# Encoder layer on one core: constant products ahead of the first loads, the first root in one run, and the last output block's sums and scalings on other engines

## The chip, the cores and the metric

The kernel runs on one core of a Trainium2 chip. The metric is the device time of one execution in microseconds (us), as the median of several runs. Five engines work side by side, each through a list of instructions of its own: TensorE (PE; its weight loads are PEld), VectorE (DVE), ScalarE (ACT), GpSimd (POOL) and SyncE (SP), which issues most of the DMAs. All data are float32; PSUM has eight banks for the results of products, and SBUF holds everything else.

## The reference

A layer of a bidirectional encoder on 2048 tokens of 1024 channels. Cut to what matters here:

```python
u = rms_norm(h, norm_mix_g) ; proj = u @ w_in        # the opening of the kernel
h = h + concat(hyena(proj), mlstm(proj)) @ w_out
h = h + cross_attention(rms_norm(h, norm_x_g), rms_norm(mem, norm_mem_g))
h = h + square(relu(rms_norm(h, norm_ff_g) @ ff_w1)) @ ff_w2
return rms_norm(h, final_norm_g)                     # the end of the kernel
```

`rms_norm(x, g)` is `x * rsqrt(mean(x * x) + eps) * g` over the 1024 channels.

## The kernel before, in words

**Products.** Every operand of a product is split into a high and a low half of a shorter type (ScalarE copies the high half, L1667 or L368, and VectorE or GpSimd subtracts it, L1668 or L368). A product of two split operands is three matmuls (`mm3`: L357 high by high, L360 and L361 with one low half each). A scheduler orders each engine's instructions from estimates of its own; an instruction given to `keep_in_program_order` (in `x_first` it is called `pin`) stays in the order of the code, and `behind` puts one behind the last product written so far.

**Opening** (`x_first`, L543 to L640, and `sweep`). The first projection needs x of 512 tokens times the gain, in halves (xh by ScalarE L574, xl by VectorE L575), for the first half x0 and then for the next 512 tokens x1. The norm's root is not applied to the operands: it multiplies the results. For it, ScalarE squares x (L580), VectorE adds the eight squares up (L582, `ssum`), TensorE adds over the channels (`columns`, L587, four products with a column of ones), VectorE takes the inverse root (`inv_rms` L462, `rsqrt` L230 to L234, a copy L463) and spreads it over a diagonal (L496), TensorE makes rows of it (`rows`, L598, ones times diagonal), ScalarE copies them (`rowb`, L599), and VectorE multiplies the results with them (L780). `sweep` makes one group of 24 products (eight k by three) after another, first two columns of the first weight block with x0, two of the second block with x0, and then the same four with x1. `self.made` counts the groups; `hooks` is a table that says before which group and k each part above is written down. L278 is the first product of the filters' small network, which runs between the groups. The halves of a later weight block are made by L368.

**Last block** (`ffn`, from L1777). The second projection of the feed-forward part uses seven products per block of 2 by 2 in place of eight. It has four blocks o of output columns; for each, the products i come in the order 1, 6, 7, 5, 3, 2, 4 (`ORDER_DOWN`), for two halves tp of the tokens, with four steps k of 12 matmuls. `fetch_a` prepares the weight side (ah, al; for i = 3 it first subtracts one block from another, L1795) and `fetch_b` the activation side (bh, bl). After the last step of a product its four banks are added to `acc[i, tp]` (L1994, VectorE). Banks come in two sets of four, `mm` for tp = 0 and `hy` for tp = 1. Only in the last block, o = 3, `add(i, j, tp, engine)` then adds the accumulators to each other (L1960), four pieces each, which makes the four output blocks of the scheme. `turned` queues the transposes of the finished blocks (L1927), whose results are squared by ScalarE (L1929) and multiplied with the final gain by VectorE (L1930), and `finish` takes the root and scales both halves of 512 tokens c (L1942 on VectorE for h = 1 and even c, L1944 on ScalarE otherwise) and stores them (L1947). The order of c is 1, 3, 0, 2; c = 0 and c = 2 end the kernel.

Of the kernel before, what the change touches and what calls it, by code (L numbers as in the profile page):

```python
# [10 lines left out]
F32 = mybir.dt.float32  # L11
# [3 lines left out]
ALU = mybir.AluOpType  # L15
# [5 lines left out]
D = 1024  # L21
# [112 lines left out]
class Prog:  # L134
# [88 lines left out]

    def rsqrt(self, pool, ms, name):
        nc = self.nc
        shp = list(ms.shape)
        y = pool.tile(shp, F32, tag=name + "_y", name=name + "_y", bufs=2)
        t = pool.tile(shp, F32, tag=name + "_t", name=name + "_t", bufs=2)
        yi, mi = y.bitcast(I32), ms.bitcast(I32)
        nc.vector.tensor_scalar(yi, mi, -0.5, float(0x5F3759DF), ALU.mult, ALU.add)  # L230
        for _ in range(3):
            nc.vector.tensor_tensor(t, y, y, ALU.mult)
            nc.vector.scalar_tensor_tensor(t, t, -0.5, ms, ALU.mult, ALU.mult)
            nc.vector.scalar_tensor_tensor(y, t, 1.5, y, ALU.add, ALU.mult)  # L234
        return y
# [222 lines left out]

    def inv_rms(self, dst, src):
        nc, sb, n = self.nc, self.isb, dst.shape[1]  # L460
        ms = sb.tile([128, 4], F32, tag="ms", name="ms", bufs=2)[:, 0:n]
        nc.vector.tensor_scalar(ms, src, 1.0 / D, EPS, ALU.mult, ALU.add)  # L462
        nc.vector.tensor_copy(dst, self.rsqrt(sb, ms, "xr"))  # L463

# [27 lines left out]

    def diagonal(self, cols):
        dg = self.isb.tile([128, 512], F32, tag="rb", name="dg", bufs=2)[:, 0:128 * cols.shape[1]]
        for t in range(cols.shape[1]):
            self.nc.vector.tensor_scalar(dg[:, 128 * t:128 * t + 128], self.ident, cols[:, t:t + 1], None, ALU.mult)  # L496
        return dg
# [50 lines left out]
    def x_first(self):  # L548
# [22 lines left out]
        def operand(xs, c, k):  # L571
            to = (slice(None), k, slice(512 * c, 512 * c + 512))
            g = self.g_mix[:, k:k + 1]
            pin(nc.scalar.activation(self.xh[to], xs[k], AF.Copy, scale=g))  # L574
            nc.vector.scalar_tensor_tensor(self.xl[to], xs[k], g, self.xh[to].bitcast(F32), ALU.mult, ALU.subtract)  # L575

        def squares(xs, c):
            for k in range(8):
                sq = sb.tile([128, 512], F32, tag="st", name="sq", bufs=3) if k else ssum[c]
                pin(nc.scalar.activation(sq, xs[k], AF.Square))  # L580
                if k:
                    nc.vector.tensor_tensor(ssum[c], ssum[c], sq, ALU.add)  # L582

        def columns(c):
            p = self.hy()
            for t in range(4):
                d = nc.tensor.matmul(p[:, t:t + 1], ssum[c][:, 128 * t:128 * t + 128], self.ones[:, 0:1], start=True, stop=True)  # L587
# [33 lines left out]

        def halfway():
            operands(range(4, 8))
            squares(x1, 1)
# [114 lines left out]
    def sweep(self, cols, hf, first, after=None):  # L739
# [3 lines left out]
        for run in [cols[:2]] + [[c2] for c2 in cols[2:]] if self.made == 0 else [[c2] for c2 in cols]:  # L743
# [7 lines left out]
            for c, c2 in [(c, c2) for c in range(2) for c2 in run]:  # L751
                wh, wl = ws[c2]
                for m in range(2):
# [5 lines left out]
                    for k in range(8):  # L759
                        if (self.made, k) in self.hooks:  # L760
                            self.hooks.pop((self.made, k))()
                            hook = True
                        else:
                            hook = False
                        self.mm3(p, wh[:, k, ms], wl[:, k, ms], xh[:, k, cs], xl[:, k, cs], k == 0, k == 7,
                                 k == 0 and 3 < self.made < 13 or hook and self.made in (2, 3))

# [1004 lines left out]
    def ffn(self):  # L1772
# [127 lines left out]
        with tc.tile_pool(name="down", bufs=1) as B:  # L1900
# [31 lines left out]
            def finish(c, dst):  # L1932
                m = B.tile([128, 4], F32, tag="mo", name="mo", bufs=2)
                q = self.rbp[:, 4 * c:4 * c + 4]
                for h in range(2):
                    nc.vector.scalar_tensor_tensor(m, ss[:, c, h], 1.0 / D, m if h else q, ALU.mult, ALU.add)
                rv = self.rsqrt(B, m, "or")
                for t in range(4):
                    for h in range(2):
                        v = dst[h][:, t]  # L1940
                        if h and c % 2 == 0:
                            nc.vector.tensor_scalar(v, v, rv[:, t:t + 1], None, ALU.mult)  # L1942
                        else:
                            nc.scalar.mul(v, v, rv[:, t:t + 1])  # L1944
# [13 lines left out]
            def add(i, j, tp, eng):  # L1958
                for m in range(4):
                    eng.tensor_tensor(acc[i, tp][:, m], acc[i, tp][:, m], acc[j, tp][:, m], ALU.add)  # L1960

            early = [(i, tp, k) for i in (7, 4, 3, 2) for tp in range(2) for k in range(4)]
            outs = []
            V, G = nc.vector, nc.gpsimd
            for s, (n, tp, k) in enumerate(down):
# [17 lines left out]
                if tp and n + 1 < len(prods):  # L1983
                    fetch_a(n + 1, k)
                for _ in range(min(len(outs), 2 if len(outs) > 4 or n + 1 == len(prods) else 1)):
                    outs.pop(0)("mm" if tp else "hy")
                if k < 3:
                    continue
                for m in range(4):
                    v = acc[i, tp][:, m]  # L1990
                    if o == 0 and i in (1, 6, 5):
                        nc.scalar.copy(v, bank[m])
                    else:
                        d = nc.vector.tensor_tensor(v, bank[m], v, ALU.add)  # L1994
                        if s + 1 == len(down):
                            tc.keep_in_program_order(d)
                if o < 3:
                    continue
# [4 lines left out]
                elif i == 7:  # L2003
                    add(7, 6, tp, V)
                    add(3, 6, tp, G)
                elif i == 5:
                    add(3, 5, tp, V)
                    add(5, 7, tp, G)
                    add(4, 7, tp, G)
                    if tp:  # L2010
                        outs += turned(1, 0, 1, 5, 1)
                elif i == 3:
                    c = 2 * tp + 1
# [3 lines left out]
                elif i == 2:  # L2017
                    outs += turned(2 * tp, tp, 0, 2, 7)
                elif i == 4:
# [129 lines left out]
```

## Time and profile before

| | us |
|---|---|
| median of 3 runs | 3109.32 (3107.85 to 3111.45) |
| profiled execution | 3110.14 |
| its span on the core | 3108.4 |
| TensorE busy | 3025.3 (97%) |
| VectorE busy | 1955.3 (63%) |
| ScalarE busy | 1497.7 (48%) |
| GpSimd busy | 1141.1 (37%) |

A row of the timeline has the start in the span, the duration, the engine, the line, the operation, what it writes and reads, shapes, how many such instructions stand in a row (x), and in brackets the idle time just before with what ended it. A row of a group has the number, the busy time, the mean duration of one in ns, and the idle time. A row of windows has the busy time of each engine in that stretch with its number of instructions, the granted clock of TensorE (PEclk, 1.00 is full), the share of the DMA engines' time and the rate. Matmuls are pipelined, so the time that one takes is read from start to start.

### The profile page before, as it was taken

How to read it: one execution, taken by the hardware profiler on the slowest of the kernel's cores; microseconds unless marked ns; L12 is line 12 of the kernel's file. 1: busy time of each engine (PE TensorE's matmuls, PEld its weight loads, DVE VectorE, ACT ScalarE, POOL GpSimd, SP SyncE). 2: the span in 40 equal slices, each digit the busy share in tenths (PEclk: the TensorE clock that was granted, in tenths of full speed). 3: DMA queues.
4: the chain of work that ended last, by engine and by line, in shares of the span. 5: the costliest groups of instructions: out<-in, count | busy, mean ns of one | idle time of the engine just before them, and what ended most of it. 6: DMA issues, size and time to landing. Idle time of an engine off the chain costs nothing.

```text
span 3108.4 us, 42926 instructions
## 1 busy us (share of the span) xinstructions
PE 3025.3 (97%) x14257; PEld 2374.5 (76%) x14257; DVE 1955.3 (63%) x3429; ACT 1497.7 (48%) x2931; POOL 1141.1 (37%) x802
## 2 busy tenths in 40 slices
PE   8999999999999998999999999999999999999998
PEld 6655667776676766888887888888888788888876
DVE  7865465446756456877664566657554676565696
ACT  6543466533656225565544455556555443333335
POOL 0122011200222333333132337766466375243693
PEclk9999999999999999999999999999999999999999
DMA  6654768576878996565476557657644565354435
GB/s 211 190 198 163 231 207 251 178 232 194 254 203 241 302 300 220 158 199 170 143 250 206 197 172 235 207 178 238 200 153 153 171 210 182 109 166 118 157 93 172
DMA packets 444102, 607.07 MB, mean 195 GB/s; under 512 B 38494, under 2 KB 248542, under 8 KB 442856
## 3 DMA queue, kind: packets, MB, share of 16 engines
q1 hardware_dynamic: 405988, 546.54, 55.2%
q10 hardware_dynamic: 37892, 57.79, 5.5%
q8 instruction: 113, 1.85, 0.2%
q14 instruction: 109, 0.89, 0.1%
HBM read 401.79 MB, written 202.41 MB: 194 GB/s over the span
## 4 chain that ended last, share of the span: by engine, by line
PE 55%; DVE 3%; DMA 1%; issue 1%; ACT 1%; POOL 0%; SPq 0%; DVEq 0%; POOLq 0%; ACTq 0%
PE mm L361 12%; PE mm L357 12%; PE mm L360 12%; PE hy L357 6%; PE hy L361 6%; PE hy L360 6%; DVE bl L1668 1%; PE hy L1310 1%; PE hy L1312 1%; DVE acc L1960 0%; PE hy L1458 0%; DVE acc L1994 0%; PE hy L1571 0%; DMA va<-vd 0%; PE hy L1272 0%
## 5 line engine op out<-in xcount | busy, mean ns | idle before, releaser
L1668 DVE TENSOR_TENSOR bl<-wr,bh 128x512 fp32r<-128x512 f32 x213 | 242.1, 1142 | 127.6 <-ACT bh L1667 122.9
L1667 ACT CAST ah<-w 128x512 fp32r<-128x512 f32 x284 | 176.5, 622 | 301.1 <-PE hy L360 155.9
L368 DVE TENSOR_TENSOR wl<-wn,wh 128x512 fp32r<-128x512 f32 (+1 forms) x296 | 213.1, 765 | 101.0 <-ACT wh L368 100.4
L357 PE MATMUL mm<-xh,wh 128*128 128x512 f32 x640 | 267.5, 419 | 8.5 <-ACT wh L368 7.9
L1024 POOL TENSOR_TENSOR b<-b,a 128x512 f32<-128x512 f32 x64 | 87.0, 1362 | 509.4 <-ACT b L1022 238.8
L360 PE MATMUL mm<-xl,wh 128*128 128x512 f32 x640 | 253.7, 397 | 1.3 <-DVE xl L368 1.3
L361 PE MATMUL mm<-xh,wl 128*128 128x512 f32 x640 | 254.8, 399 | 0.0
L1667 ACT CAST bh<-wr 128x512 fp32r<-128x512 f32 x232 | 143.5, 621 | 230.2 <-PE mm L361 172.6
L1668 DVE TENSOR_TENSOR al<-w,ah 128x512 fp32r<-128x512 f32 x236 | 216.0, 916 | 55.5 <-ACT ah L1667 54.1
L357 PE MATMUL mm<-bh,ah 128*128 128x512 f32 x576 | 225.2, 391 | 1.8 <-DVE acc L1830 1.7
L361 PE MATMUL mm<-bh,al 128*128 128x512 f32 x576 | 223.3, 390 | 2.6 <-POOL al L1668 2.6
L360 PE MATMUL mm<-bl,ah 128*128 128x512 f32 x576 | 224.4, 390 | 0.0
L368 ACT CAST wh<-wn 128x512 fp32r<-128x512 f32 (+1 forms) x296 | 164.2, 618 | 109.4 <-PE mm L361 52.7
L360 PE MATMUL mm<-act,wh 128*128 128x512 f32 x512 | 202.3, 395 | 0.0
L361 PE MATMUL mm<-act,wl 128*128 128x512 f32 x512 | 200.5, 393 | 0.9 <-DVE wl L368 0.9
L357 PE MATMUL mm<-act,wh 128*128 128x512 f32 x512 | 199.6, 396 | 1.3 <-ACT wh L368 1.2
L357 PE MATMUL hy<-bh,ah 128*128 128x512 f32 x448 | 175.2, 391 | 0.0
L360 PE MATMUL hy<-bl,ah 128*128 128x512 f32 x448 | 174.6, 390 | 0.0
L361 PE MATMUL hy<-bh,al 128*128 128x512 f32 x448 | 174.4, 390 | 0.0
L357 PEld LDWEIGHTS mm<-xh,wh 128*128 128x128 f32 x640 | 121.1, 189 | 60.8 <-issue 18.6
L357 PE MATMUL mm<-wh,xh 128*128 128x256 f32 (+1 forms) x512 | 156.0, 305 | 3.8 <-ACT xh L368 2.3
L361 PEld LDWEIGHTS mm<-xh,wl 128*128 128x128 f32 x640 | 121.0, 189 | 47.8 <-issue 23.2
(375 smaller groups left out, 8225.4 us busy)
## 6 DMA issues: line engine op xcount, KB each, us to landing
wr<-hc SPq DMA_DIRECT2D x224, 256.0 KB
w<-in_ff_w_dram SPq DMA_DIRECT2D x172, 256.0 KB
hc<-wn SPq DMA_DIRECT2D x128, 256.0 KB
wn<-in_w_in_dram SPq DMA_DIRECT2D x100, 256.0 KB
hc<-q SPq DMA_DIRECT2D x96, 256.0 KB
fs<-a SPq DMA_DIRECT2D x32, 512.0 KB
a<-fs SPq DMA_DIRECT2D x64, 256.0 KB
a<-zs SPq DMA_DIRECT2D x64, 256.0 KB
```

The costliest lines, as they stand in the source:

```text
L357: first = mm(ps, lh, rh, start=start, stop=False)
L360: mm(ps, lh, rl, start=False, stop=False)
L361: self.last = mm(ps, ll, rh, start=False, stop=stop)
L368: both = (self.nc.scalar.copy(hi, src), self.nc.vector.tensor_tensor(lo, src, hi.bitcast(F32), ALU.subtract))
L1024: nc.gpsimd.tensor_tensor(xt, xt, hi[:, m], ALU.mult)
L1310: nc.tensor.matmul(dst, nm[:, h], va[:, h], start=True, stop=state is None)
L1312: nc.tensor.matmul(dst, rows_[d, 1][:, h], state[:, h], start=False, stop=True)
L1667: self.nc.scalar.copy(hi, src)
L1668: eng.tensor_tensor(lo, src, hi.bitcast(F32), ALU.subtract)
```

## The change

**Opening.** Fifteen products of the ones matrix with itself (128x128) are written at the head of `x_first` and nothing reads them. The root of x0, from the scaling of the sums to the diagonal, is pinned, as are the later halves of x1, its additions, and the first matmul of each k in the third and fourth group. In the table of hooks, the column sums of x0 move from (2, 5) to (2, 4) and their rows from (3, 5) to (3, 1); the halves of x1 are now written as two pieces before and six behind the column sums; the squares of x1 move from (2, 6) to (3, 3), and the column sums and rows of x1 from (5, 1) and (5, 6) to (5, 5) and (6, 2).

**Last block.** The subtraction and the low half of the fourth weight block (n = 25) go from GpSimd to VectorE. `add(3, 6)` goes from GpSimd to VectorE. `add(3, 5)` is replaced: what `acc[5]` holds at the end of block o = 2 is added on GpSimd there, and in o = 3 VectorE adds each bank of that product to both accumulators. `add(4, 7)` is written down one or two products later. The scalings of c = 0 are written behind the last product's sums, and their half h = 1 moves from VectorE to GpSimd; of the last scalings, c = 2, VectorE gets one of ScalarE's four.

```diff
-        nc.vector.tensor_scalar(yi, mi, -0.5, float(0x5F3759DF), ALU.mult, ALU.add)
+        keep(nc.vector.tensor_scalar(yi, mi, -0.5, float(0x5F3759DF), ALU.mult, ALU.add))
...
+        p = self.hy()
+        for _ in range(15):
+            nc.tensor.matmul(p[:, 0:128], self.ones, self.ones, start=True, stop=True)
...
+            d = nc.vector.scalar_tensor_tensor(self.xl[to], xs[k], g, self.xh[to].bitcast(F32), ALU.mult, ALU.subtract)
+            if c and k > 1:
+                pin(d)
...
-            self.inv_rms(rx, p[:, 0:4])
-            self.dg = self.diagonal(rx)
+            keep = (lambda ins: ins) if c else pin
+            self.inv_rms(rx, p[:, 0:4], keep)
+            self.dg = self.diagonal(rx, keep)
...
-        self.hooks = {(0, 5): second, (1, 5): lambda: operands(range(4)), (2, 5): lambda: columns(0), (2, 6): halfway,
-                      (3, 5): lambda: rows(0), (5, 1): lambda: columns(1), (5, 6): lambda: rows(1), (6, 0): third}
+        self.hooks = {(0, 5): second, (1, 5): lambda: operands(range(2)), (2, 4): lambda: columns(0),
+                      (2, 5): lambda: operands(range(2, 8)), (3, 1): lambda: rows(0), (3, 3): lambda: squares(x1, 1),
+                      (5, 5): lambda: columns(1), (6, 0): third, (6, 2): lambda: rows(1)}
...
-            eng = nc.vector if n < 6 else nc.gpsimd
+            eng = nc.vector if n < 6 or n == 25 else nc.gpsimd
...
+                if scalings is None:
+                    scale(c, dst, rv)
+                else:
+                    scalings.append(lambda: scale(c, dst, rv, nc.gpsimd))
...
+                last = c == 2
...
-                        if h and c % 2 == 0:
-                            nc.vector.tensor_scalar(v, v, rv[:, t:t + 1], None, ALU.mult)
+                        if h and c % 2 == 0 or last and t == 3:
+                            eng.tensor_scalar(v, v, rv[:, t:t + 1], None, ALU.mult)
...
+                        if o == 3 and i == 5:
+                            w = acc[3, tp][:, m]
+                            nc.vector.tensor_tensor(w, bank[m], w, ALU.add)
...
+                for f in scalings or ():
+                    f()
+                scalings = None
+                if o == 2 and i == 5:
+                    add(3, 5, tp, G)
...
                     add(7, 6, tp, V)
-                    add(3, 6, tp, G)
+                    add(3, 6, tp, V)
                 elif i == 5:
-                    add(3, 5, tp, V)
                     add(5, 7, tp, G)
-                    add(4, 7, tp, G)
```

What the scheduler makes of it differs in three places; elsewhere the lists are nearly the same. The lines of the changed kernel are up to 22 higher (L587 has become L594, L598 L606, L1668 L1670, L1795 L1797, L1960 L1969, L1994 L2006, and the second sum is L2009).

First, TensorE in the opening. Here are the products around the first column sums, before (the sums are L587, of `ssum0`; mm_249 is the third group, mm_329 the fourth):

```order
L360 MATMUL mm_329<-xl_89,wh_107 128x512
L361 MATMUL mm_329<-xh_88,wl_108 128x512
L587 MATMUL hy_265<-ones_65,ssum0_99 128x1 x4
L357 MATMUL mm_249<-xh_88,wh_107 128x512
L360 MATMUL mm_249<-xl_89,wh_107 128x512
```

And now, where mm_261 is the third group:

```order
L360 MATMUL mm_261<-xl_89,wh_123 128x512
L361 MATMUL mm_261<-xh_88,wl_124 128x512
L594 MATMUL hy_274<-ones_65,ssum0_99 128x1 x4
L357 MATMUL mm_261<-xh_88,wh_123 128x512
L360 MATMUL mm_261<-xl_89,wh_123 128x512
```

Before, 78 products of the groups stand ahead of the sums, 9 between them and the rows (L598), and 9 between the rows and the first L278. Now 60 stand ahead, 15 between, and 21 behind.

Second, VectorE at the same place, as a piece of the difference. `ssum_99` belongs to x0 and `ssum_100` to x1:

```order
 L462 TENSOR_SCALAR ms<-hy 128x4
-L582 TENSOR_TENSOR ssum_100<-ssum_100,sq 128x512
 L230 TENSOR_SCALAR xr_y<-ms 128x4
-L582 TENSOR_TENSOR ssum_100<-ssum_100,sq 128x512
 L232 TENSOR_TENSOR xr_t<-xr_y 128x4
-L582 TENSOR_TENSOR ssum_100<-ssum_100,sq 128x512
 L233 SCALAR_TENSOR_TENSOR xr_t<-xr_t,ms 128x4
-L582 TENSOR_TENSOR ssum_100<-ssum_100,sq 128x512
 L234 SCALAR_TENSOR_TENSOR xr_y<-xr_t,xr_y 128x4
```

The additions of x1 stood between the small operations of the root; now they stand behind the diagonal, after six low halves of x1 and three of the results' multiplications.

Third, VectorE in the last block, from the first sum of product 5 (tp = 0) on. Before, where acc_22323 is `acc[5, 0]` and acc_22325 is `acc[3, 0]`:

```order
L1994 TENSOR_TENSOR acc_22323<-mm_26870,acc_22323 128x512
L1668 TENSOR_TENSOR bl_26988<-wr_26985,bh_26987 128x512
L1994 TENSOR_TENSOR acc_22323<-mm_26871,acc_22323 128x512
L1960 TENSOR_TENSOR acc_22325<-acc_22325,acc_22323 128x512
L1994 TENSOR_TENSOR acc_22323<-mm_26872,acc_22323 128x512
L1994 TENSOR_TENSOR acc_22323<-mm_26873,acc_22323 128x512
```

Now, where acc_22339 and acc_22341 are those two, and wr_27073 and al_27002 belong to the fourth weight block (n = 25):

```order
L2006 TENSOR_TENSOR acc_22339<-mm_26894,acc_22339 128x512
L2009 TENSOR_TENSOR acc_22341<-mm_26894,acc_22341 128x512
L1670 TENSOR_TENSOR bl_27008<-wr_27005,bh_27007 128x512
L2006 TENSOR_TENSOR acc_22339<-mm_26895,acc_22339 128x512
L2009 TENSOR_TENSOR acc_22341<-mm_26895,acc_22341 128x512
L2006 TENSOR_TENSOR acc_22339<-mm_26896,acc_22339 128x512
L2009 TENSOR_TENSOR acc_22341<-mm_26896,acc_22341 128x512
L2006 TENSOR_TENSOR acc_22339<-mm_26897,acc_22339 128x512
L2009 TENSOR_TENSOR acc_22341<-mm_26897,acc_22341 128x512
L1670 TENSOR_TENSOR bl_27033<-wr_27030,bh_27032 128x512
L1797 TENSOR_TENSOR wr_27073<-wr_27073,w_26014 128x512
L1670 TENSOR_TENSOR al_27002<-wr_26998,ah_27001 128x512
```

The first al of the fourth weight block, which was GpSimd's, stands twelfth from that sum on, behind the eight sums of both accumulators.

More of the change, by code (lines that the diff above doesn't have):

```diff
@@ L222, in bank_rsqrt, with rsqrt @@
         return y
-    def rsqrt(self, pool, ms, name):
+    def rsqrt(self, pool, ms, name, keep=lambda ins: ins):
         nc = self.nc
@@ L491, in row_stats, with diagonal @@
             yield
-    def diagonal(self, cols):
+    def diagonal(self, cols, keep=lambda ins: ins):
         dg = self.isb.tile([128, 512], F32, tag="rb", name="dg", bufs=2)[:, 0:128 * cols.shape[1]]
         for t in range(cols.shape[1]):
-            self.nc.vector.tensor_scalar(dg[:, 128 * t:128 * t + 128], self.ident, cols[:, t:t + 1], None, ALU.mult)
+            keep(self.nc.vector.tensor_scalar(dg[:, 128 * t:128 * t + 128], self.ident, cols[:, t:t + 1], None, ALU.mult))
         return dg
@@ L581, in squares @@
                 if k:
-                    nc.vector.tensor_tensor(ssum[c], ssum[c], sq, ALU.add)
+                    d = nc.vector.tensor_tensor(ssum[c], ssum[c], sq, ALU.add)
+                    if c:
+                        pin(d)
         def columns(c):
@@ L620, in operands @@
                 operand(x1, 1, k)
-        def halfway():
-            operands(range(4, 8))
-            squares(x1, 1)
         def third():
@@ L761, in sweep @@
                             self.hooks.pop((self.made, k))()
-                            hook = True
-                        else:
-                            hook = False
                         self.mm3(p, wh[:, k, ms], wl[:, k, ms], xh[:, k, cs], xl[:, k, cs], k == 0, k == 7,
-                                 k == 0 and 3 < self.made < 13 or hook and self.made in (2, 3))
+                                 k == 0 and 3 < self.made < 13 or self.made in (2, 3))
                     def leave(c=c, m=m, c2=c2, p=p, cc=cc, Ps=Ps, run=run):
@@ L1984, in ffn @@
                     fetch_a(n + 1, k)
+                if s + 4 == len(down):
+                    scalings = []
                 for _ in range(min(len(outs), 2 if len(outs) > 4 or n + 1 == len(prods) else 1)):
@@ L2012, in ffn @@
                 elif i == 3:
+                    if tp:
+                        add(4, 7, 0, G)
                     c = 2 * tp + 1
@@ L2017, in ffn @@
                 elif i == 2:
+                    if not tp:
+                        add(4, 7, 1, G)
                     outs += turned(2 * tp, tp, 0, 2, 7)
```

15 lines of the change are left out of this document (8 added, 7 removed).

## The prediction

> **What bounds the kernel now.** I read the page first, then the list of TensorE's waits, then windows and the timeline at the two ends that the change touches.
>
> ```profile
> PE 3025.3 (97%) x14257; PEld 2374.5 (76%) x14257; DVE 1955.3 (63%) x3429; ACT 1497.7 (48%) x2931; POOL 1141.1 (37%) x802
> PE mm L357 <- ACT wh L368: 9.2, 2, 7.9
> PE hy L598 <- DVE dg L496: 4.7, 1, 4.7
> PE mm L361 <- POOL al L1668: 2.6, 2, 2.4
> PE hy L1927 <- DVE acc L1994: 1.5, 1, 1.5
> ```
>
> TensorE is busy for 97% of 3108.4 us, so only its idle time and its slow time can be won. Of its waits (total, times, longest) the change can touch four: the start (7.9, set by loads), the first root (4.7), and 2.6 and 1.5 in the last output block. Busy time also hides a slow clock:
>
> ```profile
> core 0: us, PE busy (x) PEld busy (x) DVE busy (x) ACT busy (x) POOL busy (x), PEclk, DMA share, GB/s
> 7.93:12.36 4.43, 4.43 (x10) 3.47 (x11) 4.27 (x8) 4.22 (x7) 0.00 (x0) 1.00 1.07 394
> 12.36:28.00 15.64, 15.64 (x70) 12.91 (x69) 15.21 (x26) 14.93 (x27) 0.00 (x0) 1.00 1.04 384
> 35.83:40.16 4.33, 4.33 (x9) 2.77 (x9) 1.60 (x3) 0.59 (x1) 0.00 (x0) 0.52 0.00 0
> 2980.00:3000.00 20.00, 19.76 (x87) 16.06 (x86) 20.00 (x17) 6.33 (x11) 19.94 (x12) 1.00 0.22 66
> 3000.00:3020.00 20.00, 16.12 (x73) 12.67 (x72) 20.00 (x20) 6.40 (x14) 19.37 (x13) 1.00 0.40 123
> ```
>
> The first ten products take 4.43 us (0.44 each); the next 70 records take 15.64, which is 0.227 each with a few records missing. After the root's stall the same slow pace returns for 4.33 us, at a granted clock of 0.52. In the last block VectorE and GpSimd both have next to no idle time, so the ends of the waits there are queues, not latencies.
>
> **The opening.** Rows of TensorE and VectorE:
>
> ```profile
> 0.93 0.17 DVE L150 MEMSET ones<- 128x128 f32 x1
> 7.93 0.80 PE L357 MATMUL mm<-xh,wh 128*128 128x512 f32 x1 [7.93 <-ACT wh L368]
> 22.20 0.69 DVE L582 TENSOR_TENSOR ssum<-ssum,sq 128x512 f32<-128x512 f32 x1
> 28.00 0.95 PE L587 MATMUL hy<-ones,ssum 128*128 128x1 f32 x8
> 35.83 2.07 PE L598 MATMUL hy<-dg,ones 128*128 128x512 f32 x2 [4.68 <-DVE dg L496]
> 40.85 1.02 PE L278 MATMUL hy<-b,fw 66*128 66x512 f32 x2
> 47.88 0.95 PE L587 MATMUL hy<-ones,ssum 128*128 128x1 f32 x8
> 51.25 0.88 DVE L496 TENSOR_SCALAR dg<-ident,small 128x128 f32<-128x128 f32 x4
> 53.60 1.02 PE L598 MATMUL hy<-dg,ones 128*128 128x512 f32 x2
> ```
>
> The 15 constant products can begin when the ones are written, at 0.93 + 0.17 = 1.10. No row has their shape. The nearest is L598, four times as wide: 1.02 at 53.60 and 2.07 at 35.83, so one costs 0.26 to 0.52 and all of them 3.8 to 7.8, ending between 4.9 and 8.9. With 4.43 us slow and the rest fast it is 8.5 x 0.52 + 6.5 x 0.26 = 6.1, ending at 7.2, under the load wait until 7.93. Its ends: a product start delayed by 1.0 (8.9 - 7.93), or hidden altogether. If the clock stays up over the 0.7 us to 7.93, ten products cost 10 x 0.227 and **2.16** of the 4.43 goes.
>
> Then the order: 60 products stand ahead of the column sums now, so TensorE reaches them at 7.93 + 60 x 0.227 = 21.5. Their input is VectorE's last addition, which ends at 22.89, and VectorE's list up to there is unchanged: a **new wait of 1.4**. Behind it on TensorE stand only the 15 products that the root's own time covers. From column sums to diagonal an undisturbed root takes 52.13 - 47.88 = 4.25 (the second root, above); the first took 35.83 - 28.00 = 7.83 because the additions of the other half stood between its operations. In one piece it is done at 22.9 + 4.25 = 27.2. TensorE meanwhile has the sums (0.8 start to start) and 15 products, 3.4: it arrives at 27.1. The stall of 4.68 is gone, and with it the slow 4.33 us, since there is no long gap before. After L606 (0.86 start to start) come 21 products (4.8) up to the filter's L278: 27.2 + 0.9 + 4.8 = 32.9, against 40.85. That is 7.9 earlier with the same products done; counted singly, 2.16 + 4.68 + 2.1 (six to seven products and L598 at half speed, of 4.33) - 1.4 = 7.5. I take **7.5**; bounds 9.0 (no new wait) and 3.0 below.
>
> Is it kept? The additions and the xl of the second half now come after the root. They need VectorE for 6 x 0.68 + 7 x 0.6 before the second column sums, which TensorE reaches 40 products after L278, at about 42; the list ends near 39. The next weight block has slack:
>
> ```profile
> 54.22 2.50 DVE L368 TENSOR_TENSOR wl<-wn,wh 128x512 fp32r<-128x512 f32 x4 [2.10 <-ACT wh L368]
> 68.39 0.79 PE L357 MATMUL mm<-xh,wh 128*128 128x512 f32 x1
> ```
>
> Its halves are ready at 56.72 and first used at 68.39, 11.7 later, more than the 7.5 even if they come no earlier. So I give nothing back; beyond it, up to 4.5 could be lost where a later load or VectorE's list does not move along.
>
> On the clock, two gaps of this kernel:
>
> ```profile
> 1003.97 1.13 PE L1019 MATMUL hy<-a,dm 128*128 128x512 f32 x2 [2.17 <-DVE b L1023]
> 1005.93 2.04 PE L977 MATMUL hy<-b,em 128*128 128x512 f32 x2 [0.83 <-ACT a L978]
> 3010.69 0.50 PE L361 MATMUL mm<-bh,al 128*128 128x512 f32 x1 [2.35 <-POOL al L1668]
> ```
>
> A gap of 2.35 left the products fast; 2.17 and 0.83 with little between made the next pair cost 2.04, not 1.02. The Trainium skill, "TensorE: Matmul & The Clock Gate", section "What's actually happening", says that the array falls back to half clock after an idle window of about 3.4 us, rises after a busy one, and that the windows run freely, so the count of slow products varies. The row at 1005.93 disagrees with that length, or shows two gaps counted together. By the page the gaps of 0.7 and 1.4 cost nothing; by that row, they can, which is the second rival.
>
> **The last block.** Rows, then groups (count | busy, mean ns) of 2955 to 3025:
>
> ```profile
> 2869.19 1.30 POOL L1668 TENSOR_TENSOR al<-wr,ah 128x512 fp32r<-128x512 f32 x1 [12.28 <-ACT ah L1667]
> 2880.21 0.69 DVE L1668 TENSOR_TENSOR bl<-wr,bh 128x512 fp32r<-128x512 f32 x1 [1.01 <-ACT bh L1667]
> 2997.34 3.48 DVE L1668 TENSOR_TENSOR bl<-wr,bh 128x512 fp32r<-128x512 f32 x2
> 3000.73 0.68 DVE L1994 TENSOR_TENSOR acc<-mm,acc 128x512 f32<-128x512 f32 x1
> 3014.50 1.28 DVE L1994 TENSOR_TENSOR acc<-hy,acc 128x512 f32<-128x512 f32 x2
> 3015.24 0.66 PE L1927 MATMUL hy<-ident,acc 128*128 128x128 f32 x4 [1.53 <-DVE acc L1994]
> L1960 DVE TENSOR_TENSOR acc<-acc 128x512 f32<-128x512 f32 x23 | 30.1, 1328 | 0.0
> L1668 DVE TENSOR_TENSOR bl<-wr,bh 128x512 fp32r<-128x512 f32 x20 | 29.5, 1492 | 0.0
> L1960 POOL TENSOR_TENSOR acc<-acc 128x512 f32<-128x512 f32 x21 | 35.2, 1691 | 5.5 <-DVE acc L1960 5.5
> L1795 POOL TENSOR_TENSOR wr<-wr,w 128x512 f32<-128x512 f32 x4 | 6.9, 1716 | 0.1
> L1668 POOL TENSOR_TENSOR al<-wr,ah 128x512 fp32r<-128x512 f32 x4 | 6.4, 1614 | 0.0
> ```
>
> Alone, a subtraction takes VectorE 0.69 (0.6 start to start) and GpSimd 1.30; beside each other 1.74 each. A sum out of a bank takes 0.68 beside GpSimd as well. So a pair of SBUF operations goes through in 1.70, and a GpSimd operation holds VectorE up by 1.1. The Trainium skill, "SBUF — State Buffer", section "Who interferes with whom", gives the rule: a VectorE operation with two SBUF inputs contends with a GpSimd one that reads SBUF, under an exclusive lock, and one with a single SBUF input does not. The rows agree. By it alone, each move to VectorE takes away one contender and makes one longer list, so it speaks for no large gain.
>
> GpSimd loses 16 operations here (add(3,6) 8, the four subtractions and four al of the fourth weight block); add(3,5) goes from VectorE to o=2 on GpSimd: 8 x 1.30 = 10.4, in idle time like the 12.28 ahead of 2869.19, so free; if that cover were gone, the next al would be late by what sticks out, 4 x 1.30 = 5.2. VectorE up to its first sum at 3014.50 has about 61 operations x 0.6 = 36.6 of 59.5 us, so it stood still for 22.9 under some 35 operations of GpSimd x 1.1 = 38.5, that is 0.6 of them. After: 61 - 8 + 8 (add(3,6)) + 8 (second sums) + 4 + 3 = 76 x 0.6 = 45.6, and 19 of GpSimd x 1.1 x 0.6 = 12.5: 58.1 together, 1.4 less. The transposes at 3015.24 need a bank that this sum frees, so what the 2.35 and 0.24 ahead of it become matters less than this end: I take a gain of **0.7**, half of it, since the al of the fourth block now stand behind the second sums. Bounds: all of 2.6 + 1.5 = 4.1 won, or all 19 holding VectorE fully (19 x 1.1 x 0.4 = 8.4 more): 7 lost. Nothing queued behind is due earlier than those banks.
>
> **The tail.**
>
> ```profile
> 3089.67 1.68 DVE L1942 TENSOR_SCALAR acc<-acc,or_y 128x512 f32<-128x512 f32 x4
> 3091.25 2.48 DVE L1994 TENSOR_TENSOR acc<-hy,acc 128x512 f32<-128x512 f32 x4
> 3092.00 2.45 PE L1927 MATMUL mm<-ident,acc 128*128 128x128 f32 x16 [1.17 <-DVE acc L1994]
> 3102.00:3104.00 2.00, 0.00 (x0) 0.00 (x0) 0.00 (x0) 0.36 (x1) 0.00 (x0) 0.50 1.05 398
> ```
>
> The four scalings ahead of the last sums leave VectorE: 3091.25 - 3089.67 = **1.6** earlier, and transposes, root and stores follow. GpSimd has no row of a scaling; its additions say 1.30 to 1.74, so 5.2 to 7.0, done by 3096.7, and its stores, which stand ahead of the last ones on SP's queue, by 3099.3 at 398 GB/s; the last stores begin about 3099.6. From 1.8 each on it would cost. The last scalings shared 5 to 3 give 0: in that window the DMA engines are full (1.05, 398 GB/s).
>
> **Sum**: 7.5 + 0.7 + 1.6 = 9.8; the profiled execution took 3110.14 (span 3108.4), so 3100.3; the median was 0.8 lower: **3099.5**.
>
> **Rivals.** (1) The opening is partly given back: the last paragraph's 4.5 lost, 3104; for it, ACT and VectorE are full to 28; against it, 11.7 of slack. (2) The clock falls again in the gap before 7.93 or in the new wait, 2.2 each: 3101.7 or 3104; 1005.93 for, 3010.69 against. (3) The opening does not do what it says, since the column sums wait for VectorE's additions anyway: only 2.16 + 0.7 + 1.6, so 3105. (4) Slower: VectorE becomes the bound of the last block. If each of its 16 moved operations costs 1.70 and the second sums 8 x 0.6, less 8 additions at 1.33, its list grows by 27.2 + 4.8 - 10.6 = 21.4, and with no idle time there TensorE waits it out: 3099.5 + 0.7 + 21.4 = 3121.6. It decides when the sum of 3014.50 stands over 15 us later against the products around it, since 7.5 + 1.6 and the 6.2 below are then used up. Against it: GpSimd has only 19 operations left to collide with.
>
> **Chances.** Forecast 0.62 (3096 to 3102.5), rival 1 0.12, rival 2 0.10, rival 3 0.05, the milder loss of 7 there (3107) 0.06, rival 4 0.05. Run to run, about 0.2%, 6.2 us, can be told from no change: faster is below 3103.1, same to 3115.5. With half of rival 2 and a third of rival 1 below that line, faster is 0.62 + 0.05 + 0.04 = 0.71, slower 0.05, same the other 0.24. The range, 3095 to 3106, leaves out the last two cases and little of the first.
>
> **What would show it.** Products 0.227 apart from 7.93; a wait of 1.4 at the column sums; none over 1 at L606; L278 near 33; in the last block waits of about 3 in all, with GpSimd idle between operations; last sums right behind the root. It is wrong if 0.43 spacing returns, if waits grow between 40 and 120, or if VectorE's sum at 3014.5 (less the shift) is late.

## The result and the profile after

The changed kernel takes 3099.73 us (median of 6 runs, 3095.72 to 3102.64) against 3110.36 for the kernel before beside it: a ratio of 0.9966, 95% interval 0.9954 to 0.9978, or 10.6 us less (6.8 to 14.3). The forecast was 3099.5. The profiled execution took 3097.53, with a span of 3095.8, 12.6 less than before.

From the page and the list of TensorE's waits, changed kernel (total, times, longest):

```profile
PE 3023.0 (98%) x14287; PEld 2375.2 (77%) x14287; DVE 1952.6 (63%) x3442; ACT 1500.4 (48%) x2930; POOL 1130.9 (37%) x798
PE mm L361 <- DVE al L1670: 3.8, 1, 3.8
PE mm L357 <- ACT wh L368: 1.5, 2, 0.9
PE hy L594 <- DVE ssum L587: 1.1, 1, 1.1
```

The waits of 7.9 at the start and of 4.7 at the first root are gone; one of 1.1 at the column sums is new, and the three of the last block (2.6 together and 1.5) have become one of 3.8, now for VectorE. The opening on TensorE's timeline:

```profile
1.14 5.99 PE L562 MATMUL hy<-ones 128*128 128x128 f32 x30 [1.14 <-DVE ones L150]
7.73 0.50 PE L357 MATMUL mm<-xh,wh 128*128 128x512 f32 x1 [0.61 <-ACT wh L368]
22.73 1.05 PE L594 MATMUL hy<-ones,ssum 128*128 128x1 f32 x8 [1.10 <-DVE ssum L587]
27.61 1.12 PE L606 MATMUL hy<-dg,ones 128*128 128x512 f32 x2 [0.31 <-DVE dg L496]
33.37 1.02 PE L278 MATMUL hy<-b,fw 66*128 66x512 f32 x2
```

The constant products (two records each) take 5.99 and end 0.6 ahead of the first product of the layer; the column sums come after a wait of 1.1, the rows 0.3 after their turn, and the first filter product stands at 33.37, where it was 40.85. That is 7.5 earlier, the sum of the forecast. The last block, on TensorE, VectorE and ScalarE:

```profile
2989.00:3009.00 20.00, 16.17 (x70) 12.94 (x69) 17.96 (x27) 6.38 (x13) 10.06 (x9) 0.91 0.43 130
2990.71 0.69 DVE L1797 TENSOR_TENSOR wr<-wr,w 128x512 f32<-128x512 f32 x1 [1.08 <-DMA wr<-in_ff_w_dram]
2991.32 0.68 DVE L2006 TENSOR_TENSOR acc<-mm,acc 128x512 f32<-128x512 f32 x1
2999.44 0.68 DVE L1670 TENSOR_TENSOR al<-wr,ah 128x512 fp32r<-128x512 f32 x1
3000.17 0.79 PE L361 MATMUL mm<-bh,al 128*128 128x512 f32 x1 [3.83 <-DVE al L1670]
3002.04 0.63 PE L357 MATMUL mm<-bh,ah 128*128 128x512 f32 x1
3001.62 0.62 ACT L1669 CAST bh<-wr 128x512 fp32r<-128x512 f32 x1 [8.02 <-DMA wr<-hc]
```

The low half (al) that TensorE wants at 2996.3 begins at 2999.44, behind eight sums that begin at 2991.32; a subtraction ahead of those (L1797) has itself waited 1.08 for its load, with all of VectorE's list behind it. GpSimd is busy for only 10.06 of these 20 us. Behind the wait of 3.83 TensorE runs at 0.43 us a product for a while (granted clock 0.91 over the stretch). The tail:

```profile
3078.47 2.48 DVE L2006 TENSOR_TENSOR acc<-hy,acc 128x512 f32<-128x512 f32 x4
3078.65 6.20 POOL L1951 TENSOR_SCALAR acc<-acc,or_y 128x512 f32<-128x512 f32 x4 [12.25 <-DVE or_y L234]
3079.59 2.07 PE L1929 MATMUL mm<-ident,acc 128*128 128x128 f32 x16
3087.27 2.07 DVE L1951 TENSOR_SCALAR acc<-acc,or_y 128x512 f32<-128x512 f32 x5
```

The last sums begin when the root ends, the transposes follow the last product without a wait, and GpSimd's four scalings (1.55 each) are done at 3084.85, before the last ones begin at 3087.27. The last transpose is 12.8 earlier than before and the end of the span 12.6, so 0.2 of the 1.7 won in the tail goes again behind it.

To see where the 12.6 arise, I subtract the start of the same product in the profile before from that in a run (minus: earlier). The columns: the first filter product; the first use of the filters' output (near 110 us before); the last inverse transform (1017); the last transpose ahead of the feed-forward part (1814); the first second-half product of the second projection (2474); its last product (3090); and the last transpose.

| run | 41 | 110 | 1017 | 1814 | 2474 | 3090 | end |
|---|---|---|---|---|---|---|---|
| changed | -7.5 | -4.9 | -4.4 | -11.3 | -11.5 | -11.1 | -12.8 |
| after_again | -7.3 | -6.5 | -8.9 | -11.5 | -12.5 | -13.2 | -14.9 |
| open_alone | -7.3 | -5.3 | -2.8 | -8.6 | -10.2 | -10.2 | -10.2 |
| stores_other_queue | -7.2 | -5.0 | -5.2 | -6.7 | -7.7 | -8.3 | -10.0 |
| fetch_gpsimd | -6.1 | -5.8 | -6.7 | -8.0 | -9.9 | -8.0 | -9.7 |
| old_tail | -6.2 | -5.8 | -2.5 | -6.1 | -6.2 | -4.7 | -4.6 |
| low_half_early | -6.4 | -4.3 | -3.1 | -7.0 | -9.4 | -9.8 | -11.5 |
| raw_tiles_free | -6.0 | -5.1 | -4.5 | -7.0 | -8.0 | -9.9 | -11.6 |
| last_alone | +0.5 | +1.1 | +2.7 | +1.8 | +1.4 | +2.0 | +0.3 |
| no_warm | -6.2 | -2.0 | -2.4 | -4.7 | -6.2 | -6.9 | -8.6 |
| warm_alone | -0.6 | -0.6 | +1.3 | +2.8 | +2.0 | +3.4 | +3.4 |
| sums_later | -8.7 | -1.4 | -1.7 | -0.1 | -1.2 | -2.0 | -3.7 |
| both | -8.6 | -1.8 | +0.6 | -1.8 | -0.6 | -0.7 | -2.4 |

The first eight rows have one and the same order of products up to the last block. On average over them 6.7 is won in the opening, 1.4 of it (0.3 to 2.6) is lost again by 110, and 4.1 comes in the middle, where nothing was meant to change. All leads are against a single profile of the kernel before; last_alone, which has that kernel's order up to the last block, is 1.4 later at 2474.

### The profile page after: what moved, and what is told of

It is laid out like the page before. It is cut to its first block, busy times and chain, and to the rows that moved or that the text cites. A ratio compares the mean times of both kernels' runs of the same rounds, so it can differ in the third digit from the quotient of the medians.

```text
span 3095.8 us, 42982 instructions
## 1 busy us (share of the span) xinstructions
PE 3023.0 (98%) x14287; PEld 2375.2 (77%) x14287; DVE 1952.6 (63%) x3442; ACT 1500.4 (48%) x2930; POOL 1130.9 (37%) x798
## 4 chain that ended last, share of the span: by engine, by line
PE 82%; DMA 7%; DVE 5%; ACT 2%; issue 2%; POOL 1%; SPq 0%; ACTq 0%; DVEq 0%; POOLq 0%
PE mm L357 17%; PE mm L361 17%; PE mm L360 17%; PE hy L357 6%; PE hy L361 6%; PE hy L360 6%; PE hy L178 3%; PE mm L948 2%; PE hy L979 1%; PE hy L1021 1%; DMA a<-hy 1%; DMA xt<-in_x_t_dram 1%; PE hy L1312 1%; PE mm L733 1%; PE hy L1314 1%
## 5 line engine op out<-in xcount | busy, mean ns | idle before, releaser
L1670 DVE TENSOR_TENSOR bl<-wr,bh 128x512 fp32r<-128x512 f32 x213 | 238.2, 1123 | 124.7 <-ACT bh L1669 124.7
L1670 DVE TENSOR_TENSOR al<-w,ah 128x512 fp32r<-128x512 f32 x236 | 216.4, 917 | 57.1 <-ACT ah L1669 56.9
```

What stands on the lines that cost most here:

```text
L1670: eng.tensor_tensor(lo, src, hi.bitcast(F32), ALU.subtract)
```

## Experiments

Ratios are to the kernel before beside each run, with 95% intervals.

**open_alone**: the functions ahead of `ffn` from the changed kernel, `ffn` itself from before.

```diff
-            eng = nc.vector if n < 6 or n == 25 else nc.gpsimd
+            eng = nc.vector if n < 6 else nc.gpsimd
...
-                    add(3, 6, tp, V)
+                    add(3, 6, tp, G)
```

> The opening's part of the change alone, with the last block as before. The scheduler's order of the middle of the kernel is then the changed kernel's, word for word. Theory A (the reordered middle brings time of its own, as the changed kernel's trace shows between 1017 and 1801 us, where its lead grows from 4.4 to 11.3): about 11 us faster than before, the first filter product near 33.4, and again a lead of about 11 at the feed-forward part. Theory B (that lead is a matter of the single execution): 5 us faster, which is 7.5 won up to the first filter product less 2.4 given back by 110 us. Both: the waits of the last block stay at 2.4, 1.5 and 0.2.

Ratio 0.9974 (0.9964 to 0.9984), 8.1 us less. Between the two: the lead is 5.3 at 110 and grows to 10.2 by 2474. The last block neither wins nor loses: of its old waits the one for the low half is still 2.3, the one of 1.5 is gone, and six products run at half speed (shown at the end). Most of the change's gain comes with its opening, but half of that only in the middle.

**last_alone**: the opposite, the opening of before with `ffn` of the changed kernel.

```diff
-            eng = nc.vector if n < 6 else nc.gpsimd
+            eng = nc.vector if n < 6 or n == 25 else nc.gpsimd
...
+                if s + 4 == len(down):
+                    scalings = []
```

> The last block's part alone, with the opening as before; the order of the middle is that of the kernel before. Theory A (terms of the forecast): 0.7 for the sums and 1.6 for the tail, 2.3 us faster. Theory B (what the changed kernel's trace shows: a wait of 3.8 for the fourth block's low half with slow products behind it in place of 4.1 of waits, and the tail 1.7 shorter): 1.3 us faster, a wait of 3 to 4 for the low half on VectorE, half-speed products behind it. Both: nothing changes before 2950.

Ratio 0.9997 (0.9988 to 1.0006): no difference that can be told from none. The profile shows what theory B said:

```profile
3013.01 0.50 PE L361 MATMUL mm<-bh,al 128*128 128x512 f32 x1 [3.77 <-DVE al L1668]
3014.27 0.63 PE L357 MATMUL mm<-bh,ah 128*128 128x512 f32 x1
3091.58 2.48 DVE L2004 TENSOR_TENSOR acc<-hy,acc 128x512 f32<-128x512 f32 x4
```

From 2474 to the last product it loses 0.6, in the tail it wins 1.7. That nothing changes before 2950 did not hold: the same order of products drifts against the other profile, between 1.5 earlier (near 1110) and 4.0 later (near 1150), so single profiles of the middle differ by that much by chance.

**no_warm** and **warm_alone**: the changed kernel without the constant products, and the kernel before with only them.

```diff
-        for _ in range(15):
-            nc.tensor.matmul(p[:, 0:128], self.ones, self.ones, start=True, stop=True)
```

> The changed kernel without the 15 constant products. Theory A (the slow start costs its own time): first ten products in 4.4 us again, first filter product 2.2 later, at 35.5. Theory B (the column sums wait for VectorE's additions anyway, 1.1 in the changed kernel): the wait of 1.1 at the column sums goes and only 1.1 is lost, first filter product near 34.5. The scheduler's order of the middle may change with it; what comes after the first filter product is not this run's question.

> The kernel before with only the 15 constant products added. Theory A: the first products run at full speed, 2.2 us are won at the column sums and kept, first filter product at 38.7. Theory B (the root is held by the additions of the second half on VectorE, which wait for ScalarE's squares): the stall at the rows grows by what is won, and the first filter product stays between 39.5 and 40.9; total 0 to 1.4 faster.

TensorE without them, and then the kernel before with them:

```profile
24.12 0.95 PE L591 MATMUL hy<-ones,ssum 128*128 128x1 f32 x8
28.89 1.13 PE L603 MATMUL hy<-dg,ones 128*128 128x512 f32 x2 [0.25 <-DVE dg L496]
34.65 1.02 PE L278 MATMUL hy<-b,fw 66*128 66x512 f32 x2
```

```profile
25.85 0.94 PE L590 MATMUL hy<-ones,ssum 128*128 128x1 f32 x8
35.35 2.07 PE L601 MATMUL hy<-dg,ones 128*128 128x512 f32 x2 [6.34 <-DVE dg L496]
40.25 1.02 PE L278 MATMUL hy<-b,fw 66*128 66x512 f32 x2
```

Theory B both times. Without them the wait at the column sums is gone and the first filter product is 1.3 later (34.65 for 33.37), not 2.2. With them alone the column sums are 2.15 earlier, the stall at the rows grows from 4.68 to 6.34, and 0.6 is left. Behind the opening each has an order of its own: no_warm's ratio is 0.9990 (0.9981 to 0.9999), and warm_alone is slower than before, 1.0011 (1.0002 to 1.0020), so theory B's total of 0 to 1.4 faster fell. Only the stretch up to the first filter product measures the constant products.

**after_again**: the changed kernel unaltered.

> The changed kernel unaltered, for a second profile and as the measure of the next three. Theory A (the lead won between 1017 and 1801 belongs to the order of the products there): it grows by about 7 again. Theory B (it is chance, as the copy of the old order in the run with the last block alone drifted by up to 4 us either way): it grows by some other amount, 0 to 4. Both: first filter product at 33.4, lead 5 at 110, one wait of 3 to 4 in the last block, tail 1.7 shorter.

Ratio 0.9968 (0.9957 to 0.9979), 3097.34 us. The lead grows by 2.6 between 1017 and 1814 here and by 6.9 in the first profile, so theory A's number fell and theory B's held. Over 110 to 2474 the eight profiles of this order gain 6.6, 6.0, 4.9, 2.7, 4.1, 0.4, 5.1 and 2.9, 4.1 on average, while last_alone, sums_later and both lose 0.3, 0.2 and 1.2. That points to the order, with chance of some 3 either way; warm_alone loses 2.6 and no_warm gains 4.2 with orders of their own. Which swap in it brings the time was not tried.

TensorE's granted clock varies between 1017 and 1814 too. A window of 300 us there, first of the kernel before and then, 6 us earlier, of the changed one (the 0.94 and 0.96 are the clock):

```profile
1050.00:1350.00 300.00, 271.79 (x1343) 215.48 (x1340) 190.62 (x535) 133.56 (x413) 104.21 (x77) 0.94 0.72 235
1044.00:1344.00 300.00, 273.62 (x1372) 216.75 (x1371) 191.92 (x536) 135.67 (x418) 105.84 (x78) 0.96 0.73 240
```

The four profiles with 0.96 or 0.97 there (changed, open_alone, old_tail, low_half_early) gain 3.6 to 6.9 between 1017 and 1814; the other nine in the table have 0.94 or 0.95 and gain at most 2.6 or lose up to 1.6. All four have the changed order, but so do four of the nine. So part of the middle goes with the granted clock, which varies within one order; whether the clock makes the time or both follow from the waits there stays open.

**fetch_gpsimd**: the fourth block's fetch back on GpSimd.

```diff
-            eng = nc.vector if n < 6 or n == 25 else nc.gpsimd
+            eng = nc.vector if n < 6 else nc.gpsimd
```

> The changed kernel with the fourth weight block's subtraction and low half back on GpSimd. Theory A (in the changed kernel VectorE's list is what is late: it waits twice for that block's loads, 1.1 each, and does four second sums ahead of the low half, while GpSimd stands idle for 3.0 and 5.7): the wait of 3.8 falls below 1, no product behind it runs at half speed, 4 to 5 us faster than the changed kernel. Theory B (GpSimd is late there as it was before): a wait of 2 to 4 on GpSimd's low half, within 1 us of the changed kernel.

The stretch of the last block, and the wait in it:

```profile
2989.00:3009.00 20.00, 16.17 (x62) 12.73 (x61) 14.91 (x21) 5.55 (x10) 20.00 (x15) 0.83 0.42 132
3000.19 4.20 POOL L1670 TENSOR_TENSOR al<-wr,ah 128x512 fp32r<-128x512 f32 x3
3001.96 0.79 PE L361 MATMUL mm<-bh,al 128*128 128x512 f32 x1 [3.83 <-POOL al L1670]
```

Theory B: the same wait of 3.83, now with GpSimd busy for all of the 20 us and VectorE for 14.91. Ratio 0.9971 (0.9960 to 0.9983).

**old_tail**: the scalings ahead of the last sums and shared as before.

```diff
-                if s + 4 == len(down):
-                    scalings = []
...
-                        if h and c % 2 == 0 or last and t == 3:
+                        if h and c % 2 == 0:
```

> The changed kernel with the scalings of the last two blocks of tokens as before, ahead of the last sums and shared as before; nothing else. Forecast's step: 1.6 us slower than the changed kernel, the last sums 1.6 after the root's end. Rival: the last stores hold the end anyway, no difference.

```profile
3085.02 1.67 DVE L1951 TENSOR_SCALAR acc<-acc,or_y 128x512 f32<-128x512 f32 x4
3086.61 2.48 DVE L2004 TENSOR_TENSOR acc<-hy,acc 128x512 f32<-128x512 f32 x4
3087.35 2.45 PE L1929 MATMUL mm<-ident,acc 128*128 128x128 f32 x16 [1.17 <-DVE acc L2004]
```

The sums stand 1.59 behind the root's end again, and the tail wins nothing (-4.7 to -4.6 in the table), where each profile with the new tail wins 1.7. As a whole 0.9976 (0.9967 to 0.9985), 2.5 us above after_again by the ratios, within their intervals.

**stores_other_queue**: the stores of the projected tiles from ScalarE's queue.

```diff
-                nc.sync.dma_start(out=dst[:, 4 * j4:4 * j4 + 4], in_=st[0:w])
+                (nc.scalar if self.made < 16 else nc.sync).dma_start(out=dst[:, 4 * j4:4 * j4 + 4], in_=st[0:w])
```

> The changed kernel with the stores of the projected tiles issued from ScalarE's queue in place of SyncE's during the first 16 groups; the products' order is unaltered. Theory A (the 2.5 us given back between 75 and 110 come from those stores: they stand behind a load that waits on SyncE's queue, ScalarE waits 4.5 for a free tile, and the casts of a weight block behind it come late): no wait of TensorE near 91, lead at 110 about 7 in place of 5. Theory B (the data path is full there, or the results' own chain sets the pace): lead at 110 stays at 5.

This asked about three rows of the changed kernel, the SyncE queue, ScalarE and TensorE:

```profile
86.43 5.43 SPq L824 DMA_DIRECT2D hy<-st  x2
90.94 0.59 ACT L206 COPY st<-mm 126x512 f32<-126x512 f32 x1 [4.48 <-DMA hy<-st]
91.58 0.50 PE L357 MATMUL mm<-xh,wh 128*128 128x512 f32 x1 [1.28 <-ACT st L206]
```

TensorE's waits from 70 to 110 with the other queue:

```profile
PE hy L281 <- ACT b L263: 0.8, 1, 0.8
PE mm L357 <- ACT st L206: 0.6, 1, 0.6
```

The wait of 1.28 falls to 0.6, but one of 0.8 for the filters' chain stands beside it, and the lead at 110 is 5.0 all the same. Theory A fell. Ratio 0.9974 (0.9963 to 0.9986).

**sums_later**: the hooks six products later. **low_half_early**: two low halves on GpSimd ahead of `add(5, 7)`, both pinned there. **both** is the two together.

```diff
-        self.hooks = {(0, 5): second, (1, 5): lambda: operands(range(2)), (2, 4): lambda: columns(0),
-                      (2, 5): lambda: operands(range(2, 8)), (3, 1): lambda: rows(0), (3, 3): lambda: squares(x1, 1),
+        self.hooks = {(0, 5): second, (1, 5): lambda: operands(range(2)), (2, 6): lambda: columns(0),
+                      (2, 7): lambda: operands(range(2, 8)), (3, 3): lambda: rows(0), (3, 5): lambda: squares(x1, 1),
```

```diff
+            if n == 25 and k < 2:
+                hi, lo = (self.R.tile([128, 512], F32R, tag=t, name=t, bufs=4) for t in ("ah", "al"))
+                nc.scalar.copy(hi, src)
+                tc.keep_in_program_order(nc.gpsimd.tensor_tensor(lo, src, hi.bitcast(F32), ALU.subtract))
+                aq[n, k] = hi, lo
+                return
...
-                    eng.tensor_tensor(acc[i, tp][:, m], acc[i, tp][:, m], acc[j, tp][:, m], ALU.add)
+                    d = eng.tensor_tensor(acc[i, tp][:, m], acc[i, tp][:, m], acc[j, tp][:, m], ALU.add)
+                    if i == 5:
+                        tc.keep_in_program_order(d)
...
-                    add(5, 7, tp, G)
                     if tp:
+                        add(5, 7, 0, G)
+                        add(5, 7, 1, G)
```

> The changed kernel with the first column sums, the rows and the squares behind them written six products later each, so that TensorE has work until VectorE's last addition. Theory A: the wait of 1.1 at the column sums goes, the root is ready at the same time and the 15 products still cover it, first filter product 1.1 earlier (32.3), and no half-speed products behind the column sums, which two of six profiles of the unaltered order had. Theory B (the root's end decides as before): first filter product stays at 33.4 and the wait moves to the rows.

> The changed kernel, but the low halves of the first two steps of the fourth weight block are made on GpSimd, ahead of add(5, 7) there, while their subtractions stay on VectorE. Theory A (what stops TensorE in the last block is only that the low half stands behind the eight sums of two accumulators on VectorE): the wait of 3 to 4 goes, at most 1.5 comes up two steps later, no half-speed products there; 2 to 4 us faster than the changed kernel from 2474 to the last product. Theory B (the engines' lists are full, whoever does it): the wait comes back at the next thing in the list, gain below 1.

> Both alterations together, as a candidate for a faster version. Theory A: what the two give apart, 3 to 5 us below the changed kernel (3093 to 3096). Theory B: the middle of the kernel drifts by as much from one scheduler's order to another, so that no difference from the changed kernel can be told.

sums_later, its first filter product and TensorE's waits from 60 to 130:

```profile
22.94 0.97 PE L594 MATMUL hy<-ones,ssum 128*128 128x1 f32 x8
32.16 1.02 PE L278 MATMUL hy<-b,fw 66*128 66x512 f32 x2
PE hy L281 <- ACT b L263: 2.4, 2, 2.1
PE mm L821 <- ACT st L206: 1.0, 1, 1.0
```

Theory A for the opening, to a tenth: no wait at the sums, first filter product at 32.16. And yet the ratio is 0.9996 (0.9987 to 1.0006): by 110 the lead of 8.7 has shrunk to 1.4, among other things in waits for the filters' small network (L281) and for the tiles, and the middle brings nothing. low_half_early (0.9969, 0.9957 to 0.9980), at the place of the old wait:

```profile
3005.24 0.66 PE L1935 MATMUL hy<-ident,acc 128*128 128x128 f32 x2 [3.23 <-DMA wr<-hc]
3001.89 0.62 ACT L1669 CAST bh<-wr 128x512 fp32r<-128x512 f32 x1 [7.10 <-DMA wr<-hc]
```

The wait for the low half is gone and one of 3.23 stands a little later: theory B, with 0.3 won from 2474 to the last product. ScalarE's row shows what is late ahead of it, a load of the activations, for which ScalarE also waited in the changed kernel (8.02) and in the kernel before (5.87). both is 0.9993 (0.9982 to 1.0004); theory A fell for it.

**raw_tiles_free**: raw activations and raw weights share six tiles. Here two products' weights go elsewhere, on top of low_half_early.

```diff
-                src = self.raw(w[i == 4][1])
+                if n in (25, 26):
+                    src = self.WD[k, n - 24]
+                    nc.sync.dma_start(out=src, in_=w[0][1])
+                else:
+                    src = self.raw(w[i == 4][1])
```

> The run with the low halves early, and besides the raw weight blocks of the last block's fifth and sixth products are loaded into the weight tiles that the third and fourth product have left, so that they no longer take four of the six raw tiles from the activations. Theory A (what is late in the last block, before and after the change, is the activations' loads, which wait for a raw tile: ScalarE waits 6 to 8 there for a load): the wait of 3.2 goes and none over 1 comes in its place, no half-speed products, about 3 us won from 2474 to the last product against the run with the low halves early; ScalarE's wait for that load falls below 4. Theory B (VectorE's list is the bound whatever the loads do): a wait of 2 to 4 comes back on VectorE's low half or on the sums.

The stretch, and TensorE's waits from 2945 to 3095:

```profile
2989.00:3009.00 20.00, 18.07 (x85) 14.69 (x84) 20.00 (x24) 6.54 (x13) 17.24 (x12) 1.00 0.36 103
PE hy L1939 <- DMA wr<-hc: 1.9, 1, 1.9
PE mm L361 <- POOL al L1670: 0.8, 1, 0.8
```

Each theory half: from 2474 to the last product it wins 1.9, where low_half_early won 0.3 (one profile each), ScalarE no longer waits for those loads, and the clock stays up. What is left of the waits, 2.7, comes with VectorE at 20.00 of 20. (The name of the load in the wait is the last event seen; that load had long arrived here, and VectorE's first sum out of the bank, at 3004.96, was the late one.) The total, 3098.72 and 0.9968 (0.9955 to 0.9980), cannot be told from the changed kernel's: no version here beats it measurably.

## Why the prediction was right, and where it was not

The total was right, and partly by luck: two steps of the sum promised too much, and a gain in the middle, which the sum did not have, made up for them.

- **The opening up to the first filter product**: right in mechanism, and 7.5 for 7.5 in the first profile, with the new wait at 1.1 (1.4 forecast) and the rows' wait at 0.3; 7.2 to 7.5 in four profiles of this order and 6.0 to 6.4 in the other four. The constant products took 5.99 (6.1), and 5.1 to 6.5 over the eight. Worth noting is what they are worth: 2.16 in the sum, but 1.3 in this order and 0.6 in the old one, since VectorE's additions come next. Against the average of the eight, no_warm is only 0.5 later: it has no wait at the column sums, and so none of the slow products that follow that wait in four of the eight.
- **"So I give nothing back"**: wrong. Rival 1 came in part: 0.3 to 2.6 go again by 110 in the profiles of this order, 1.4 on average. The slack of 11.7 that I quoted was one weight block's. In the first profile 1.8 of the 2.6 are waits that the kernel before did not have, 1.3 for the copy of a projected tile and 0.5 for the filters' network. What holds them was not found: with the stores on another queue the lead at 110 stayed at 5.0. sums_later shows the same on a larger scale: 7.3 of 8.7 lost.
- **Rival 2, the clock in the new wait**: it happened, in 4 of the 8 profiles of this order (below), at 1.1 on average at the first filter product, not 2.2. At 110 these four lead by 5.3 and the others by 5.4, so there it no longer counts.
- **The middle**: no step of the forecast. 4.1 on average came from there, and only that makes the total fit: 5.3 at 110, 4.1, about 0 in the last block and 1.7 in the tail are 11.1, against 10.6 measured. That is luck. That the 4.1 belongs to the order is likely and not shown; part of it goes with the granted clock.
- **The last block's sums, 0.7**: near 0. The profiles with these sums and the low half behind them change by +0.4, -0.7, -0.6, +1.6, +0.6, -0.8 and -0.6 from 2474 to the last product (changed, after_again, stores_other_queue, old_tail, last_alone, sums_later, no_warm). The count of operations on VectorE was read too high (53 start between 2955 and its sum of 3014.50, not about 61), but the 15 more came out (68). VectorE did not become the bound of the block, as rival 4 had it: its first second-half sum, of hy, stands at 3003.48 for 3014.50, by 11.0 earlier as everything around it. But I had the transposes as the bound, and it was the low half that came late, which I had named and only halved the gain for: a wait of 3.0 to 3.8 in place of 4.1, with half-speed products behind it in three of the seven. The raw tiles, which raw_tiles_free points to as part of that, were in no step.
- **The tail, 1.6**: right, 1.7 at the last transpose and 1.5 at the end of the span.

## What to carry to other kernels

A gain at the head of a program is worth what is left of it where the next chains meet: take it at several later points of the same two profiles, not at the first. Where a scheduler places the rest, an edit in one place moves the order everywhere, and the middle here changed by 4.1 on average with no edit in it; compare variants only up to the point where their orders part, and repeat profiles before explaining a few microseconds between them. When a wait moves unchanged from engine to engine, look for what they share: here part of it seems to be a ring of six tiles, seen in ScalarE's wait for a load.

## What the runs showed of the hardware

Whether a short wait costs TensorE its clock varies from run to run. fetch_gpsimd, behind the column sums:

```profile
23.07 1.05 PE L594 MATMUL hy<-ones,ssum 128*128 128x1 f32 x8 [1.19 <-DVE ssum L587]
24.76 0.58 PE L357 MATMUL mm<-xh,wh 128*128 128x512 f32 x1
25.56 0.63 PE L361 MATMUL mm<-xh,wl 128*128 128x512 f32 x1
```

A wait of 1.0 to 1.3 there, with 0.8 of one-column products behind it, was followed by half-speed products in fetch_gpsimd, old_tail, low_half_early and raw_tiles_free, and in the other four profiles of this order it was not; the four that were have a first filter product about 1.1 later on average.

In the last block the length of the wait does not decide it alone. After 3.8 (changed kernel, old_tail, last_alone, fetch_gpsimd) and 3.2 (low_half_early, both) some products ran at half speed. After about 3.1 they did in warm_alone and did not in after_again, stores_other_queue, sums_later and no_warm. After 2.35 they did not in the kernel before, and after 2.32 they did in open_alone:

```profile
3000.51 0.50 PE L361 MATMUL mm<-bh,al 128*128 128x512 f32 x1 [2.32 <-POOL al L1670]
3002.20 0.63 PE L361 MATMUL mm<-bh,al 128*128 128x512 f32 x1
```

The Trainium skill, "TensorE: Matmul & The Clock Gate", section "What's actually happening", puts the fall behind an idle window of about 3.4 us in windows that run freely. The free run agrees with the chance in both places; the length of 3.4 does not fit a fall after 2.3 or after 1.2.
